# One more step of lookahead in the down stage of a feed-forward, with squares written later and the powers of the norm begun sooner

## The chip, the core and the metric

The kernel runs on one core of a Trainium2 chip. The core has TensorE (PE: matmuls and transposes, 128 x 128 weights against up to 512 columns), VectorE (DVE), ScalarE (ACT), GpSimd (POOL) and SyncE (SP, which issues loads and stores). Each engine works through a queue of its own in order, and a semaphore holds an instruction until what it needs is there. The metric is the device time of one execution in microseconds, the median of several runs.

## The reference

512 tokens of width 1024 pass through two layers. A layer is a feed-forward, a group of four token mixers, and a second feed-forward, each behind an RMS norm and added to x:

```python
def rmsnorm(x, g):
    xf = x.astype(jnp.float32)
    y = xf * lax.rsqrt(jnp.mean(xf * xf, axis=-1, keepdims=True) + EPS)
    return (y * g.astype(jnp.float32)).astype(x.dtype)

def swiglu(h, w1, w3, w2):
    return (jax.nn.silu(h @ w1) * (h @ w3)) @ w2

for l in range(DEPTH):                       # DEPTH = 2
    h = rmsnorm(x, ffn1_norm[l])
    x = x + FFN_RESIDUAL * swiglu(h, ffn1_w1[l], ffn1_w3[l], ffn1_w2[l])   # 0.5; w2 is 2816 x 1024
    h = rmsnorm(x, mix_norm[l])
    ...                                      # four token mixers, added to x
    h = rmsnorm(x, ffn2_norm[l])
    x = x + FFN_RESIDUAL * swiglu(h, ffn2_w1[l], ffn2_w3[l], ffn2_w2[l])
return rmsnorm(x, final_norm)
```

## The kernel before

**Stages.** The four feed-forwards are called f0a, f0b, f1a and f1b (layer, first or second). Each has an up stage (w1 and w3 with the gate) and a down stage (w2). After f0a and f1a come the mixers of the layer (L0, L1), after f1b the last norm and the store. x is held as four blocks of 128 tokens, x0 to x3.

**Precision.** Every float32 product is made of three: an operand is split into a rounded part, hi, by a cast on ScalarE, and the rest, lo, by a subtraction on VectorE, and TensorE adds hi·hi, hi·lo and lo·hi (lines 107 to 109). So each piece of weights costs a cast whi, a split wlo, and for the activations a cast and a split `as`, all before its matmuls can start.

**The down stage.** The product with w2 is cut into halves of tokens and of output columns and made with seven products in place of eight, called a to g, whose operands are quarters of w2 or sums of them. A quarter has 11 rows of 128, taken in six pieces j (`SUB`: five of two rows, one of one). So there are 42 steps (product, piece), in the order a0 a1 b0 a2 b1 ... b5, d and e in the same way, c and f in the same way, then g0 to g5. A full step is 12 matmuls of 512 columns, one with the last piece 6.

Before a step's matmuls three things happen to its weights. `fetch` has SyncE load a raw quarter piece into one of six places (tag `raw`, shared with the up stage). `presum` adds on VectorE what is a sum: for b the raw pieces of a and b into a tile tt, for c the raw pieces c and h, for f the activations. `prepare` makes the splits, whi and wlo into three places each. For b and d it also has GpSimd issue an accumulating load onto tt, which makes the weights of a later product. In the loop over steps s the calls are `fetch(s + 6)`, `presum(s + 4)`, `prepare(s + 2)`, `product(s)`, `joins(s)`.

`joins(s)` adds finished products from PSUM (tiles px, pz, pw, pr) to x, half the columns of a block at a time (`add`), has ScalarE square what of x is final and sum it by rows (`square`), and begins the next norm: `scale` adds the two sums of squares (nv, VectorE), raises that to −1/2 (ry, GpSimd, `rsqrt`) and scales the block (xn, VectorE). Behind g3 the blocks 2 and 3 are transposed on TensorE (`turn`, pt; in f1b there is no norm to feed, and no transpose). Then g4 and g5 are done for one block of tokens after the other, each followed by its add, square and `scale` (in f1b by `last`, which scales and stores).

**What sets the order.** Within a down stage the order on VectorE and ScalarE is that of the calls (`manual_schedule`), and so it is on TensorE in the whole program. `s_` and `sn` in the tables are operands of the gate of the up stage, `raw_f0a9..` and `wlo_f0a9..` weights of its last step.

Of the kernel before, what the change touches and what calls it, by code (L numbers as in the profile page):

```python
# [15 lines left out]
P = 128  # L16
# [33 lines left out]
def trunk(ctx: ExitStack, tc: tile.TileContext, x, par, gains, tab, w13, w2, wi, wg, wo, out):  # L50
# [61 lines left out]
    def rsqrt(v, n, name):  # L112
        y = small.tile([P, n], F32, tag=f"ry{n}", name=f"ry_{name}")
        G.tensor_tensor(y, v, expo[:, 0:n], ALU.pow)
        return y


    class Norm:
# [3 lines left out]
        def __init__(self, name, index):  # L122
            self.name, self.index = name, index
            self.quarters = index % 3 != 1
            self.ss, self.xn = {}, {}
            self.gain = None
            self.op = {}
            self.t = {}
# [11 lines left out]

        def scale(self, b):
            with tc.high_priority(offset=400):
                if self.gain is None:
                    self.gain = first_gain if self.index == 0 else load_gain(self.index)
                v = small.tile([P, 1], F32, tag="nv", name=f"nv_{self.name}{b}", bufs=4)
                ss = self.ss[b]
                V.tensor_scalar(v, ss[:, 0:1], ss[:, 1:2], EPS, ALU.add, ALU.add)
                y = rsqrt(v, 1, f"{self.name}{b}")
                xn = tmp.tile([P, D], F32, tag="xn", name=f"xn_{self.name}{b}")
                V.scalar_tensor_tensor(xn, xt[b], y, self.gain, ALU.mult, ALU.mult)  # L150
                self.xn[b] = xn
# [219 lines left out]
    def down(f, a, s1, s2, nxt, name, end=False):  # L371
# [53 lines left out]
        def prepare(s):  # L425
# [16 lines left out]
            raw = tview(j) if m in "bdf" else raws[m, j]  # L442
            whi = wts.tile([P, n, T], F32R, tag="whi", name=f"whi_{name}{m}{j}")
            wlo = wts.tile([P, n, T], F32R, tag="wlo", name=f"wlo_{name}{m}{j}")
            S.copy(whi, raw)
# [31 lines left out]
        def joins(s):  # L477
# [5 lines left out]
            elif (m, j) == ("d", 0):  # L483
                for t in range(2):
                    add(1, 1, t, "z", 1)
            elif (m, j) == ("d", last):
                for t in range(2):
                    add(0, 1, t, "x", -1)
            elif (m, j) == ("c", 1):
                for t in range(2):  # L490
                    add(0, 0, t, "w", 1)
                    nxt.square(t, 0)
            elif (m, j) == ("c", last):
                for t in range(2):
                    add(1, 1, t, "x", -1)
                    nxt.square(2 + t, 1)
                    add(1, 0, t, "x", 1)
            elif (m, j) == ("f", last):
                for t in range(2):
                    add(1, 0, t, "r", 1)  # L500
                    nxt.square(2 + t, 0)
            elif m == "g" and j < 2:
                if end:
                    nxt.last(2 + j)
                else:
                    nxt.scale(2 + j)

        with tc.manual_schedule(engines={mybir.EngineType.DVE, mybir.EngineType.Activation}):
            for s in range(6):
                fetch(s)  # L510
            for s in range(2):
                prepare(s)
            for s in range(2, 4):
                presum(s)
            tail = len(steps) - 2
            for s in range(tail):
                fetch(s + 6)
                presum(s + 4)
                prepare(s + 2)
                product(s)  # L520
# [4 lines left out]
            for t in range(2):  # L525
                for s in (tail, tail + 1):
                    product(s, (t,))
                add(0, 1, t, "z", 1)
                nxt.square(t, 1)
                if end:  # L530
                    nxt.last(t)
# [427 lines left out]
```

## Time and profile before

| what | value |
|---|---|
| median of three runs | 1709.82 us |
| the three runs | 1709.77, 1709.82, 2012.91 us |
| profiled execution, its own time | 1710.36 us |
| its span in the trace | 1708.7 us |
| busy, share of the span: PE, PEld, DVE, ACT, POOL | 97%, 89%, 77%, 50%, 8% |
| chain that ended last, by engine | PE 83%, DVE 10%, issue 3%, ACT 3%, DMA 1% |
| mean DMA rate | 166 GB/s |

The profile shows one execution. Busy shares are taken over the whole span. A matmul's record overlaps the next one, so its start is the surer time. In the chain of waits each piece is followed back to what released it; "issue" is time in which an engine waited for nothing that the profile shows. The run of 2012.91 us stands alone.

### The profile page before, as it was taken

Reading aid. Unit: us, or ns where it says so; the run is one execution under the profiler, and the core shown is the slowest. Engines: PE = TensorE matmul, PEld = TensorE weight load, DVE = VectorE, ACT = ScalarE, POOL = GpSimd, SP = SyncE. Lnnn points to the kernel's source line nnn. Section 1 sums busy time; section 2 is a strip of 40 time slices with the busy share of each in tenths; the row PEclk is TensorE's granted clock in tenths of the full one; section 3 lists DMA queues with packets and bytes.
Section 4 is the critical chain, followed back from the end, with each engine's and each line's share of the span. In section 5 each row is a group of like instructions: output and inputs, shape, how many; then the busy total and the mean of one; then the engine's idle time right before and its main releaser. Section 6 shows DMA issues by size and latency. Waiting matters only on the chain.

```text
span 1708.7 us, 27504 instructions
## 1 busy us (share of the span) xinstructions
PE 1661.4 (97%) x11072; PEld 1517.7 (89%) x11072; DVE 1310.9 (77%) x1661; ACT 850.0 (50%) x1238; POOL 140.2 (8%) x170
## 2 busy tenths in 40 slices
PE   8999999989999999999999999999999999999997
PEld 8999998778779999988699999886887799999875
DVE  5777778879856777788887777888796577777986
ACT  5454555553344554556554554555433455545554
POOL 1000002010010001001000000010000101000100
PEclk9999999999999999999999999999999999999999
DMA  6776669543332777769457777694323346776872
GB/s 199 190 181 173 174 173 263 179 154 100 111 86 71 183 194 185 183 191 258 131 137 182 191 183 190 186 258 160 124 89 97 87 122 183 181 186 181 228 220 82
DMA packets 80479, 283.94 MB, mean 166 GB/s; under 512 B 8928, under 2 KB 9056, under 8 KB 80352
## 3 DMA queue, kind: packets, MB, share of 16 engines
q1 hardware_dynamic: 61920, 217.18, 38.7%
q0 software_dynamic: 18432, 65.02, 21.9%
q8 instruction: 86, 1.41, 0.3%
q14 instruction: 41, 0.34, 0.1%
HBM read 280.07 MB, written 2.10 MB: 165 GB/s over the span
## 4 chain that ended last, share of the span: by engine, by line
PE 83%; DVE 10%; issue 3%; ACT 3%; DMA 1%; POOL 0%; POOLq 0%; ACTq 0%; DVEq 0%; SPq 0%
PE pi_L L108 3%; PE pi_L L107 3%; PE pi_L L109 3%; PE px_f1b L109 3%; PE px_f1a L109 3%; PE px_f0a L109 3%; PE px_f1b L107 3%; PE px_f1a L107 3%; PE px_f0a L107 3%; PE px_f0a L108 3%; PE px_f1b L108 3%; PE px_f1a L108 3%; PE px_f0b L109 3%; PE px_f0b L107 3%; PE px_f0b L108 3%
## 5 line engine op out<-in xcount | busy, mean ns | idle before, releaser
L107 PE MATMUL pi_L<-gh_m,whi_L1i 128*128 128x512 f32 (+1 forms) x128 | 47.5, 371 | 0.3 <-ACT gh_m L183 0.3
L107 PE MATMUL pi_L<-gh_m,whi_L0i 128*128 128x512 f32 (+1 forms) x128 | 47.5, 371 | 0.3 <-ACT gh_m L183 0.3
L108 PE MATMUL pi_L<-gl_m,whi_L0i 128*128 128x512 f32 (+1 forms) x128 | 46.6, 364 | 0.6 <-DVE gl_m L184 0.6
L108 PE MATMUL pi_L<-gl_m,whi_L1i 128*128 128x512 f32 (+1 forms) x128 | 46.6, 364 | 0.6 <-DVE gl_m L184 0.6
L109 PE MATMUL pi_L<-gh_m,wlo_L1i 128*128 128x512 f32 (+1 forms) x128 | 46.4, 363 | 0.0
L109 PE MATMUL pi_L<-gh_m,wlo_L0i 128*128 128x512 f32 (+1 forms) x128 | 46.4, 363 | 0.0
L770 DVE SCALAR_TENSOR_TENSOR scr_gv_L<-scr_cv_L,pt,scr_gv_L 128x511 f32<-128x511 f32 (+29 forms) x60 | 43.8, 731 | 0.6
L770 DVE SCALAR_TENSOR_TENSOR scr_cv_L<-scr_cv_L,pt,scr_cv_L 128x511 f32<-128x511 f32 (+29 forms) x60 | 43.7, 728 | 0.1
L107 PEld LDWEIGHTS pi_L<-gh_m,whi_L0i 128*128 128x128 f32 x128 | 24.2, 189 | 4.9 <-ACT gh_m L183 0.6
L108 PEld LDWEIGHTS pi_L<-gl_m,whi_L1i 128*128 128x128 f32 x128 | 24.2, 189 | 4.8 <-DVE gl_m L184 0.8
L108 PEld LDWEIGHTS pi_L<-gl_m,whi_L0i 128*128 128x128 f32 x128 | 24.2, 189 | 4.8 <-DVE gl_m L184 0.8
L107 PEld LDWEIGHTS pi_L<-gh_m,whi_L1i 128*128 128x128 f32 x128 | 24.2, 189 | 4.8 <-ACT gh_m L183 0.6
L97 ACT CAST whi_L1i<-raw_L1i 128x1024 fp32r<-128x1024 f32 x14 | 14.6, 1050 | 27.3 <-PE pi_L L108 16.4
L97 ACT CAST whi_L0i<-raw_L0i 128x1024 fp32r<-128x1024 f32 x14 | 14.6, 1049 | 27.3 <-PE pi_L L108 16.4
L109 PEld LDWEIGHTS pi_L<-gh_m,wlo_L1i 128*128 128x128 f32 x128 | 24.2, 189 | 3.8
L109 PEld LDWEIGHTS pi_L<-gh_m,wlo_L0i 128*128 128x128 f32 x128 | 24.2, 189 | 3.8
L136 ACT ACTIVATE sq_a<-x 128x512 f32<-128x512 f32 x16 | 10.1, 632 | 29.3 <-DVE x L475 29.2
L205 DVE TENSOR_TENSOR B_b<-pt_b,B_b 128x512 fp32r<-128x512 f32 x16 | 10.1, 681 | 18.5 <-ACT B_b L204 18.5
L108 PE MATMUL p_f0b<-B_b,whi_f0b 128*128 128x256 f32 x64 | 19.4, 303 | 2.9 <-DVE B_b L205 2.9
L136 ACT ACTIVATE sq_m<-x 128x512 f32<-128x512 f32 x16 | 10.1, 632 | 24.0 <-DVE x L475 23.9
L108 PE MATMUL p_f1b<-B_b,whi_f1b 128*128 128x256 f32 x64 | 19.0, 298 | 2.8 <-DVE B_b L205 2.8
L107 PE MATMUL p_f0b<-B_b,whi_f0b 128*128 128x256 f32 x64 | 19.2, 300 | 2.5 <-ACT B_b L204 2.5
(3183 smaller groups left out, 7303.2 us busy)
## 6 DMA issues: line engine op xcount, KB each, us to landing
raw_L0i<-wi SPq DMA_DIRECT2D x14, 512.0 KB, 3.7
raw_L1i<-wi SPq DMA_DIRECT2D x14, 512.0 KB, 3.7
tt_f0a<-w POOLq DMA_DIRECT2D x10, 512.0 KB, 7.2
tt_f0b<-w POOLq DMA_DIRECT2D x10, 512.0 KB, 7.8
tt_f1a<-w POOLq DMA_DIRECT2D x10, 512.0 KB, 7.6
tt_f1b<-w POOLq DMA_DIRECT2D x10, 512.0 KB, 8.4
gain<-gains SPq DMA_DIRECT2D x7, 512.0 KB, 4.1
raw_L0o<-wo SPq DMA_DIRECT2D x6, 512.0 KB, 3.9
```

What stands on the lines that cost most here:

```text
L97: S.copy(hi, raw)
L107: PE.matmul(ps, sh, mh, start=first, stop=False, skip_group_check=more)
L108: PE.matmul(ps, sh, ml, start=False, stop=False, skip_group_check=more)
L109: PE.matmul(ps, sl, mh, start=False, stop=last, skip_group_check=more)
L136: S.activation(sq, xt[b][:, c * T : (c + 1) * T], AF.Square, scale=1.0 / 32.0, accum_out=self.ss[b][:, c : c + 1],)
L205: V.tensor_tensor(lo[:, :, s], ps[q], hi[:, :, s].bitcast(F32), ALU.subtract)
L770: V.scalar_tensor_tensor(acc[:, kk:], v[:, : T - kk], cw, acc[:, kk:], ALU.mult, ALU.add)
```

## The change

- The split weights of every fourth step (s % 4 == 3) go to a fourth place, the tile `q3` of another pool, which holds an operand of the up stage before. `prepare` works three steps ahead, `fetch` seven and `presum` five; the raw places stay six.
- At the start three steps are prepared instead of two, and the first sums (of b) stand ahead of them.
- The add of w moves from c1 to c2, its squares to c3. After c's last step both pairs of adds come together, and their squares follow f's last but one step. After f's last step both adds come first, then the squares.
- `scale` is cut in two, `root` (sum and power) and the scaling. For blocks 2 and 3 both roots are called at g0 and both scalings at g1. At the end of the stage the root of block 0 is called ahead of block 1's last matmuls, and both scalings (or `last`) come behind those.
- The powers have four places.

```diff
--- before.py
+++ after.py
@@ -110,7 +110,7 @@
 
 
     def rsqrt(v, n, name):
-        y = small.tile([P, n], F32, tag=f"ry{n}", name=f"ry_{name}")
+        y = small.tile([P, n], F32, tag=f"ry{n}", name=f"ry_{name}", bufs=4)
         G.tensor_tensor(y, v, expo[:, 0:n], ALU.pow)
         return y
 
@@ -122,7 +122,7 @@
         def __init__(self, name, index):
             self.name, self.index = name, index
             self.quarters = index % 3 != 1
-            self.ss, self.xn = {}, {}
+            self.ss, self.y, self.xn = {}, {}, {}
             self.gain = None
             self.op = {}
             self.t = {}
@@ -138,16 +138,22 @@
                     accum_out=self.ss[b][:, c : c + 1],
                 )
 
-        def scale(self, b):
+        def root(self, b):
+
             with tc.high_priority(offset=400):
                 if self.gain is None:
                     self.gain = first_gain if self.index == 0 else load_gain(self.index)
                 v = small.tile([P, 1], F32, tag="nv", name=f"nv_{self.name}{b}", bufs=4)
                 ss = self.ss[b]
                 V.tensor_scalar(v, ss[:, 0:1], ss[:, 1:2], EPS, ALU.add, ALU.add)
-                y = rsqrt(v, 1, f"{self.name}{b}")
+                self.y[b] = rsqrt(v, 1, f"{self.name}{b}")
+
+        def scale(self, b):
+            if b not in self.y:
+                self.root(b)
+            with tc.high_priority(offset=400):
                 xn = tmp.tile([P, D], F32, tag="xn", name=f"xn_{self.name}{b}")
-                V.scalar_tensor_tensor(xn, xt[b], y, self.gain, ALU.mult, ALU.mult)
+                V.scalar_tensor_tensor(xn, xt[b], self.y[b], self.gain, ALU.mult, ALU.mult)
                 self.xn[b] = xn
 
         def turned(self, b, q):
@@ -440,8 +446,13 @@
             t = asplits[-1]
             hi, lo = (t[:, s % 2, x, : n * 256].rearrange("p (n t) -> p n t", n=n) for x in range(2))
             raw = tview(j) if m in "bdf" else raws[m, j]
-            whi = wts.tile([P, n, T], F32R, tag="whi", name=f"whi_{name}{m}{j}")
-            wlo = wts.tile([P, n, T], F32R, tag="wlo", name=f"wlo_{name}{m}{j}")
+            if s % 4 == 3:
+
+                w = acts.tile([P, 2, n, T], F32R, tag="q3", name=f"w_{name}{m}{j}")
+                whi, wlo = w[:, 0], w[:, 1]
+            else:
+                whi = wts.tile([P, n, T], F32R, tag="whi", name=f"whi_{name}{m}{j}")
+                wlo = wts.tile([P, n, T], F32R, tag="wlo", name=f"wlo_{name}{m}{j}")
             S.copy(whi, raw)
             S.copy(hi, src)
             V.tensor_tensor(wlo, raw, whi.bitcast(F32), ALU.subtract)
@@ -486,37 +497,47 @@
             elif (m, j) == ("d", last):
                 for t in range(2):
                     add(0, 1, t, "x", -1)
-            elif (m, j) == ("c", 1):
+            elif (m, j) == ("c", 2):
                 for t in range(2):
                     add(0, 0, t, "w", 1)
+            elif (m, j) == ("c", 3):
+                for t in range(2):
                     nxt.square(t, 0)
             elif (m, j) == ("c", last):
                 for t in range(2):
                     add(1, 1, t, "x", -1)
+                for t in range(2):
+                    add(1, 0, t, "x", 1)
+            elif (m, j) == ("f", last - 1):
+                for t in range(2):
                     nxt.square(2 + t, 1)
-                    add(1, 0, t, "x", 1)
             elif (m, j) == ("f", last):
                 for t in range(2):
                     add(1, 0, t, "r", 1)
+                for t in range(2):
                     nxt.square(2 + t, 0)
-            elif m == "g" and j < 2:
-                if end:
-                    nxt.last(2 + j)
-                else:
-                    nxt.scale(2 + j)
+            elif (m, j) == ("g", 0):
+                for t in range(2):
+                    nxt.root(2 + t)
+            elif (m, j) == ("g", 1):
+                for t in range(2):
+                    if end:
+                        nxt.last(2 + t)
+                    else:
+                        nxt.scale(2 + t)
 
         with tc.manual_schedule(engines={mybir.EngineType.DVE, mybir.EngineType.Activation}):
-            for s in range(6):
+            for s in range(7):
                 fetch(s)
-            for s in range(2):
+            for s in range(2, 5):
+                presum(s)
+            for s in range(3):
                 prepare(s)
-            for s in range(2, 4):
-                presum(s)
             tail = len(steps) - 2
             for s in range(tail):
-                fetch(s + 6)
-                presum(s + 4)
-                prepare(s + 2)
+                fetch(s + 7)
+                presum(s + 5)
+                prepare(s + 3)
                 product(s)
                 joins(s)
             if not end:
@@ -527,6 +548,9 @@
                     product(s, (t,))
                 add(0, 1, t, "z", 1)
                 nxt.square(t, 1)
+                if t == 0:
+                    nxt.root(t)
+            for t in range(2):
                 if end:
                     nxt.last(t)
                 else:
```

The matmuls are the same in the same order. VectorE's queue at the entry of f0a's down stage: `wlo_f0a9..`, `s5_f0a9` belong to the last step of the up stage, `tt0` is the first sum for b, `raw_f0aa1`, `raw_f0ab1` loads of pieces of a and b. Before:

```order
L349 TENSOR_TENSOR sn_f0a9_2615<-pw_f0a9_2613,sn_f0a9_2615 128x512
L99 TENSOR_TENSOR wlo_f0a9e_2739<-raw_f0a9e_2607,whi_f0a9e_2737 128x1024
L312 TENSOR_TENSOR a04_f0a_225<-sn_f0a9_2615 128x256
L99 TENSOR_TENSOR wlo_f0a9f_2770<-raw_f0a9b_2605,whi_f0a9f_2768 128x1024
L99 TENSOR_TENSOR wlo_f0a9g_2801<-raw_f0a9g_2610,whi_f0a9g_2799 128x1024
L356 TENSOR_TENSOR s5_f0a9_2616<-px_f0a9_2612,s5_f0a9_2616 128x512
L447 TENSOR_TENSOR wlo_f0aa0_2853<-raw_f0aa0_2839,whi_f0aa0_2852 128x1024
```

After, where the sums `tt0` (b0 and b1) stand ahead of f's split of the last up step and of `s5`:

```order
L318 TENSOR_TENSOR a04_f0a_225<-sn_f0a9_2615 128x256
L425 TENSOR_TENSOR tt0_f0a_2834<-raw_f0aa0_2839,raw_f0ab0_2843 128x1024
L99 TENSOR_TENSOR wlo_f0a9f_2770<-raw_f0a9b_2605,whi_f0a9f_2768 128x1024
L99 TENSOR_TENSOR wlo_f0a9g_2801<-raw_f0a9g_2610,whi_f0a9g_2799 128x1024
L425 TENSOR_TENSOR tt0_f0a_2834<-raw_f0aa1_2841,raw_f0ab1_2847 128x1024
L362 TENSOR_TENSOR s5_f0a9_2616<-px_f0a9_2612,s5_f0a9_2616 128x512
L458 TENSOR_TENSOR wlo_f0aa0_2857<-raw_f0aa0_2839,whi_f0aa0_2856 128x1024
```

Before, both sums came behind the first splits of a; what now stands behind them is the rest of the last up step.

ScalarE's queue in f0a from f's last cast on: `sq_m0xy` is the square of block x, columns y, for the mixers' norm, `whi_L0g0` the mixers' first weights. Before:

```order
L445 CAST whi_f0af5_3559<-tt2_f0a_2836 128x512
L446 CAST as_f0af4_3538<-a15_f0a_232 128x256
L136 ACTIVATE sq_m021_3573,ss_m02_3572<-x2_83 128x512
L136 ACTIVATE sq_m031_3578,ss_m03_3577<-x3_84 128x512
L445 CAST whi_f0ag0_3584<-raw_f0ag0_3493 128x1024
L446 CAST as_f0ag0_3583<-s_f0a0_974 128x512
L445 CAST whi_f0ag1_3604<-raw_f0ag1_3515 128x1024
L446 CAST as_f0ag0_3583<-s_f0a1_1438 128x512
L136 ACTIVATE sq_m020_3617,ss_m02_3572<-x2_83 128x512
L97 CAST whi_L0g0_3787<-raw_L0g0_3785 128x1024
L136 ACTIVATE sq_m030_3620,ss_m03_3577<-x3_84 128x512
L445 CAST whi_f0ag2_3623<-raw_f0ag2_3536 128x1024
```

After:

```order
L456 CAST w_f0af5_3539<-tt2_f0a_2836 128x512
L457 CAST as_f0af4_3518<-a15_f0a_232 128x256
L456 CAST whi_f0ag0_3559<-raw_f0ag0_3467 128x1024
L457 CAST as_f0ag0_3558<-s_f0a0_974 128x512
L456 CAST whi_f0ag1_3577<-raw_f0ag1_3495 128x1024
L457 CAST as_f0ag0_3558<-s_f0a1_1438 128x512
L136 ACTIVATE sq_m021_3596,ss_m02_3595<-x2_83 128x512
L136 ACTIVATE sq_m031_3599,ss_m03_3598<-x3_84 128x512
L456 CAST whi_f0ag2_3602<-raw_f0ag2_3516 128x1024
L457 CAST as_f0ag2_3601<-s_f0a2_1902 128x512
L97 CAST whi_L0g0_3777<-raw_L0g0_3775 128x1024
L136 ACTIVATE sq_m020_3616,ss_m02_3595<-x2_83 128x512
```

The squares of the columns 1 stood ahead of the cast for g0 and stand now behind that for g1; the cast for the mixers stands behind that for g2.

VectorE's queue in f0a about the norm of blocks 2 and 3 (`nv`, `xn`). Before:

```order
L447 TENSOR_TENSOR wlo_f0ag2_3624<-raw_f0ag2_3536,whi_f0ag2_3623 128x1024
L448 TENSOR_TENSOR as_f0ag2_3622<-s_f0a2_1902,as_f0ag2_3622 128x512
L147 TENSOR_SCALAR nv_m02_3643<-ss_m02_3572 128x1
L150 SCALAR_TENSOR_TENSOR xn_m02_3647<-x2_83,ry_m02_3645,gain1_3641 128x1024
L447 TENSOR_TENSOR wlo_f0ag3_3650<-raw_f0ag3_3557,whi_f0ag3_3649 128x1024
L448 TENSOR_TENSOR as_f0ag2_3622<-s_f0a3_2366,as_f0ag2_3622 128x512
L147 TENSOR_SCALAR nv_m03_3667<-ss_m03_3577 128x1
L150 SCALAR_TENSOR_TENSOR xn_m03_3671<-x3_84,ry_m03_3669,gain1_3641 128x1024
L447 TENSOR_TENSOR wlo_f0ag4_3675<-raw_f0ag4_3581,whi_f0ag4_3674 128x1024
```

After:

```order
L458 TENSOR_TENSOR w_f0ag3_3620<-raw_f0ag3_3537,w_f0ag3_3620 128x1024
L459 TENSOR_TENSOR as_f0ag2_3601<-s_f0a3_2366,as_f0ag2_3601 128x512
L148 TENSOR_SCALAR nv_m02_3639<-ss_m02_3595 128x1
L148 TENSOR_SCALAR nv_m03_3643<-ss_m03_3598 128x1
L458 TENSOR_TENSOR wlo_f0ag4_3649<-raw_f0ag4_3556,whi_f0ag4_3648 128x1024
L459 TENSOR_TENSOR as_f0ag4_3647<-s_f0a4_2830,as_f0ag4_3647 128x512
L156 SCALAR_TENSOR_TENSOR xn_m02_3666<-x2_83,ry_m02_3641,gain1_3637 128x1024
L156 SCALAR_TENSOR_TENSOR xn_m03_3668<-x3_84,ry_m03_3645,gain1_3637 128x1024
```

Both sums now come ahead of g4's split, and both scalings behind it, one after the other.

## Rows read from the trace of the kernel before

**Rows 1.** Windows, f0a by pairs of products: us, busy (instructions) by engine, granted clock, DMA:

```profile
248.18:279.17 30.99, 30.65 (x135) 24.71 (x134) 28.01 (x36) 17.36 (x25) 6.11 (x7) 1.00 0.88 256
279.17:309.08 29.91, 29.91 (x133) 24.77 (x132) 24.58 (x31) 17.43 (x25) 4.37 (x5) 1.00 0.98 240
309.08:343.82 34.74, 32.85 (x137) 24.94 (x135) 30.91 (x41) 20.28 (x33) 0.00 (x0) 1.00 0.45 141
343.82:364.03 20.21, 17.52 (x80) 13.36 (x79) 16.75 (x23) 11.17 (x19) 2.83 (x3) 1.00 0.70 221
```

**Rows 2.** Windows of the down stages f0b, f1a and f1b:

```profile
745.52:859.92 114.40, 111.11 (x481) 87.79 (x479) 98.69 (x126) 67.27 (x102) 11.50 (x14) 1.00 0.69 194
1089.10:1205.27 116.17, 111.99 (x480) 89.00 (x479) 100.67 (x128) 66.66 (x102) 13.12 (x15) 0.99 0.73 211
1585.87:1699.48 113.61, 109.83 (x464) 85.81 (x462) 95.99 (x123) 62.57 (x95) 11.50 (x15) 1.00 0.66 185
```

**Rows 3.** Chain of waits in f0a: start, us, what:

```profile
358.35 1.75 PE pt_m L157 x16
```

**Rows 4.** Timeline of TensorE in f0a, around f0 and g0:

```profile
320.19 0.39 PE L109 MATMUL px_f0a<-whi_f0ac,as_f0af 128*128 128x512 f32 x1
...
323.04 0.39 PE L107 MATMUL pr_f0a<-whi_f0af,as_f0af 128*128 128x512 f32 x1
...
341.34 0.39 PE L109 MATMUL pr_f0a<-whi_f0af,as_f0af 128*128 128x512 f32 x1
...
343.82 0.40 PE L107 MATMUL pz_f0a<-whi_f0ag,as_f0ag 128*128 128x512 f32 x1
```

**Rows 5.** Timeline of ScalarE in f0a, from f to g (in brackets: idle before, releaser):

```profile
318.36 0.63 ACT L136 ACTIVATE sq_m<-x 128x512 f32<-128x512 f32 x1 [4.45 <-DVE x L475]
...
319.75 1.03 ACT L445 CAST whi_f0af<-tt_f0a 128x1024 fp32r<-128x1024 f32 x1
...
340.53 1.03 ACT L445 CAST whi_f0ag<-raw_f0ag 128x1024 fp32r<-128x1024 f32 x1
...
346.93 1.05 ACT L97 CAST whi_L0g<-raw_L0g 128x1024 fp32r<-128x1024 f32 x1 [0.35 <-DMA raw_L0g<-wg]
```

**Rows 6.** Timeline of VectorE in f0a, before f:

```profile
315.91 1.21 DVE L447 TENSOR_TENSOR wlo_f0ac<-raw_f0ac,whi_f0ac 128x1024 fp32r<-128x1024 f32 x1
317.05 0.68 DVE L448 TENSOR_TENSOR as_f0af<-a_f0a,as_f0af 128x512 fp32r<-128x512 f32 x1
317.65 1.28 DVE L475 SCALAR_TENSOR_TENSOR x<-pw_f0a,x 128x512 f32<-128x512 f32 x2
```

**Rows 7.** Timeline of VectorE at the end of f1b:

```profile
1697.62 0.69 DVE L475 SCALAR_TENSOR_TENSOR x<-pz_f1b,x 128x512 f32<-128x512 f32 x1 [1.06 <-PE pz_f1b L109]
...
1700.05 1.28 DVE L150 SCALAR_TENSOR_TENSOR xn_a<-x,ry_a,gain 128x1024 f32<-128x1024 f32 x1 [0.73 <-POOL ry_a L114]
...
1703.72 1.28 DVE L150 SCALAR_TENSOR_TENSOR xn_a<-x,ry_a,gain 128x1024 f32<-128x1024 f32 x1 [0.73 <-POOL ry_a L114]
```

**Rows 8.** Timeline of GpSimd, powers of the norm after f0a:

```profile
364.94 0.55 POOL L114 TENSOR_TENSOR ry_m<-nv_m,expo 128x1 f32<-128x1 f32 x1 [8.39 <-DVE nv_m L147]
368.81 1.39 POOL L114 TENSOR_TENSOR ry_m<-nv_m,expo 128x1 f32<-128x1 f32 x1 [3.32 <-DVE nv_m L147]
```

**Rows 9.** Timeline of SyncE's queue, VectorE and TensorE at f0a's entry:

```profile
233.36 0.33 SPq L91 DMA_DIRECT2D raw_f0ab<-w  x1
...
237.88 1.23 DVE L99 TENSOR_TENSOR wlo_f0a9f<-raw_f0a9b,whi_f0a9f 128x1024 fp32r<-128x1024 f32 x1 [1.37 <-ACT whi_f0a9f L97]
...
245.30 0.28 PE L107 MATMUL px_f0a<-T_n,whi_f0a9g 128*128 128x256 f32 x1
```

**Rows 10.** DMA issues from 233 to 234: KB, us to landing:

```profile
raw_f0ab<-w SPq DMA_DIRECT2D x1, 512.0 KB, 4.5
```

**Rows 11.** Tile raw_f0aa, six loads:

```profile
DMA to landing us min/median/max: 3.4/4.1/8.4
```

**Rows 12.** Window in g of f1a:

```profile
1192.93:1196.33 3.40, 3.40 (x9) 2.63 (x9) 2.81 (x3) 0.88 (x2) 0.56 (x1) 0.50 0.65 190
```

## Prediction

> **What bounds the kernel now.** I read the windows of the four down stages first, because all edits but the one at the very end lie in them. In each, TensorE is busy for 110 to 112 of 114 to 116 us, and no other engine passes 101 (for f0a the sum of its four rows) [rows 1, 2]: the matmuls are the bound, and the question is only what they lose. Busy time hides that, since a matmul's record (0.39 us) is longer than the distance to the next, so I go by starts. For f0a the windows are cut by pairs of products: a/b, d/e, c/f and g. The pair d/e runs 132 matmuls in 29.91 us without a wait, which is a pace of 0.2266. A stage has 462, so 104.69 us, and three of the four have 16 transposes as well, 1.75 [rows 3]. Against that:
>
> f0a 115.85 − 104.69 − 1.75 = 9.41; f0b 114.40 − 106.44 = 7.96; f1a 116.17 − 106.44 = 9.73; f1b, without transposes, 113.61 − 104.69 = 8.92 [rows 1, 2]. Together **36.0 us** are lost, and that is the most that the stages can give back.
>
> By pairs in f0a: a/b loses 30.99 − 29.91 = 1.08; c/f, whose window reaches three matmuls into g, 34.74 − 29.91 − 0.68 = 4.15; g the remaining 4.18. The timeline of TensorE shows two of these waits in full: from the last matmul of c's first steps to the fourth of f's first step 2.85 us pass where four paces (0.91) would do, a loss of **1.94**; from f's end to the fourth matmul of g's first step 2.48, a loss of **1.57** [rows 4].
>
> ScalarE's timeline says why. The cast of f's weights, which TensorE is waiting for, starts at 319.75, behind two squares (the first at 318.36), for which ScalarE had waited 4.45 us on an add of VectorE. The cast of g's first weights starts at 340.53, again behind squares. In g, the cast of the weights of the following mixer (346.93) waited for its load, with g's third cast queued behind it [rows 5]. So these are not engines short of time but queues in which something late stands ahead of something wanted, with only two products (24 matmuls, 5.44 us) of work prepared ahead to cover it.
>
> **The change part by part.** It adds and removes no matmul, cast, split or transfer. An add or a square is 0.6 to 0.7 us whether early or late [rows 5, 6], and nothing here costs time of its own.
>
> *Fourth place, preparing three steps ahead.* Cover goes from 24 to 36 matmuls, 8.16 us, so 2.72 more before a late split is felt. The place is the tile of the up stage's operand T4, so its first cast waits for the last up product, over at 248.18 [rows 1], and is due 36 matmuls later: no cost. Each wait above is under 3: f 1.94, g0 1.57, and in g 4.18 for two waits together. On its own that takes off most of each.
>
> *Squares and adds moved.* The add of w goes one step of c on and its squares another one; by then f's first casts are past, which removes what stood at 318.36 [rows 5]. The squares after c's last step go behind f's last but one, so they no longer stand ahead of g's first cast. Their cost stays hidden behind ScalarE's idle time: it is busy for 20.28 of 34.74 in c/f [rows 1]. If that cover were gone, one square would delay one cast by 0.7.
>
> *Norm begun sooner.* The sums and powers of blocks 2 and 3 are issued at g's first step and used one step later. On VectorE 0.2 for a sum moves ahead of g's fifth split, and the power has that split (1.14 + 0.60 from the starts in [rows 6]) to run beside. What remains is VectorE's own work between the end of c and the transposes: four adds (0.60 each, two of them take 1.28 [rows 6]), g's splits 1 to 4 at 1.74, two adds of r, the mixer's split 1.14, two sums 0.3 (one with its hand-overs is under 2.43 − 0.60 − 0.70 − 0.73 = 0.40, by the round in [rows 7]) and the scaling of block 2, 1.28 [rows 7]: 2.4 + 6.96 + 1.2 + 1.14 + 0.3 + 1.28 = 13.3. TensorE in the meantime has f's last two steps and four of g, 2.72 + 1.36 + 10.88 = 14.96. A margin of 1.7 is thin, for VectorE catches up hardly at all in c/f: a pair of steps costs it 2 × 1.74 + 1.14 + 0.60 = 5.22 per 5.44 of TensorE, and the adds of w (1.2) come on top. I allow a wait of **1.0 at each of the three turns**, between 0 (margin kept) and 3.0 (VectorE comes to the four adds behind by those of w and two splits, 1.2 + 3.48 = 4.7, and the margin takes 1.7 of it). This is what is late next. On SyncE one load of the mixer's weights moves ahead of a table's, on GpSimd in f1a one power (0.55) ahead of the issue of an accumulating load; in the stage nothing waits for what is put behind them.
>
> Speaking against it is one more row: a power alone on GpSimd takes 0.55, beside a split on VectorE it took 1.39 [rows 8], and both now run beside a split. The first needs 1.39 of 1.74, the second 2.78 of the 2.94 until its scaling, so at this price both stay hidden, and the sum holds nothing for it. The Trainium skill ("SBUF — State Buffer", section "Who interferes with whom") says that a VectorE instruction with two SBUF inputs contends with a GpSimd instruction that reads SBUF, and that whoever comes first can block the other wholly. The row agrees that it slows; it was not blocked until the split's end and 0.55 more. If it were, each turn would come some 0.8 later and the total would be some 2.4 higher.
>
> *First sums of b placed ahead of the first splits.* This adds waits. The sum of b0 now stands in VectorE's queue ahead of the split of the up stage's product f, that of b1 ahead of s5, the last but one gate's operand. In f0a the load that b0 needs is issued at 233.36 and lands 4.5 later [rows 9, 10], at 237.9, when that split would start (237.88): split and everything behind it move by 1.17. The load for b1 needs the place that this split frees, so it is issued at about 240.25; with a landing time L, sum and s5 are done at 240.25 + L + 1.14 + 0.60 + 0.1, and TensorE's last up product into X, which overwrites what s5 reads, wants to start at 245.30 [rows 9]. The wait is L − 3.2: at L = 4.1, the middle for this ring [rows 11], 0.9; at 3.4, 0.2. For it the 1.08 of a/b goes, which was a wait for the split of b0. I take **0.8** left in f0a and in f1a, whose entries look alike, and 0.1 in f0b and f1b, where the trace has the first of these loads landed before the split is due: 1.8 in all.
>
> *End.* The sum of block 1's last piece no longer stands behind the scaling of block 0. Before: add 1697.62, scaling of block 0 at 1700.05 (2.43 for add, square, sum and power), scaling of block 1 at 1703.72 [rows 7]. After, the last add can start when the matmuls end, 1699.5 to 1699.7, and 2.43 later, at 1702.1 to 1702.2, its scaling, by when that of block 0 is over. **1.5** less; 0 if the store binds.
>
> *Sum.* 36.0 lost; 1.8 stays at the entries, 3.0 at the turns, and 0.4 a stage (1.6) that I count as no wait, most of what c/f keeps in f0a when f and g0 are taken off (4.15 − 1.94 − 1.57 = 0.64). Gain 36.0 − 6.4 + 1.5 = 31.1. The profiled execution took 1710.36, so 1679.3; it was 0.54 above the median, so **1679** against 1709.82.
>
> **The rivals.** *Half of it.* Only the order of the queues helps: f and g0 go, (1.94 + 1.57) × 4 = 14.0, plus 1.5 at the end, so 1694. For it: the loads still share six places, and a step fetched sooner waits for its place; and in g a cast stood behind a load [rows 5], which more places don't bring sooner. Against: loads of this ring land in 4.1 at the middle [rows 11], less than the 8.16 ahead.
>
> *Slower: the entry.* The wait L − 3.2 in all four stages. It decides at the point where it eats a stage's gain of 7.4: L = 10.6. At 12 it costs 8.8 × 4 = 35, so 1679 + 35 = 1714. For it: a load of this ring took 8.4 [rows 11]. Against: the two in question land in less than half of 10.6.
>
> *It doesn't do what it says.* The third step ahead is prepared no sooner, since its weights aren't there or VectorE is late by as much, and the moved adds make waits of their own: the end's 1.5 and the wait of f in two of the stages (3.9) go, so 1704.
>
> *The clock.* In g of f1a TensorE was granted 0.50, its level of 1.2 GHz, for 3.40 us right behind a wait [rows 12], which is 1.7 lost; f0a's like wait passed without it. The sum has this 1.7 among f1a's 9.73. It comes back if the clock falls elsewhere: plus or minus 1.7, no case by itself.
>
> **How the numbers follow.** The forecast, 1674 to 1687, 0.74: at the lower end no turn waits and no entry does (−4.8), at the upper one turns keep 3.0 (6.0 more) and the two entries wait for an L of 4.5 (1.3 each, 1.0 more). The half, 1688 to 1699, 0.15. Not what it says, 1700 to 1711, 0.07. Slower through the entry, over 1711, 0.04. The range, 1674 to 1697, holds nearly all of the first and most of the second. A difference of 2%, 34 us, is about what a measurement of this kernel can tell from no change: faster than that is under 1675.6, and even all 36.0 with the end would give 1672, so 0.07; slower by over 2% needs an L above 19, 0.02; within, 0.91.
>
> **What would show it.** Right: stages of 107 to 109 us, c/f without a wait above 0.5, squares on ScalarE with casts of f and g ahead of them, at the turns a wait of under 1.5 with VectorE as the releaser, scaling of block 1 within 2.7 of the last matmul. Wrong: a cast of f or g that starts after TensorE came to wait for it; a product of the last up step waiting on s5 by more than 1; a power of over 1.5.

## Result

The changed kernel takes 1681.21 us, median of four runs (1680.16 to 1681.79), against 1710.67 of the kernel before (four runs, one of them the lone 2012.91, which is left out of the ratio). The ratio is **0.9824, interval 0.981 to 0.9837**: 29.5 us less. The forecast was 1679, the range 1674 to 1697. The profiled execution took 1681.03, its span is 1679.3. The prediction takes 2% for about what a measurement can tell; the four runs here lie within 1.7 us of each other, so 29.5 is told apart easily.

The windows of the four down stages, from the first matmul to the last (columns as in [rows 1]):

```profile
248.37:356.68 108.31, 107.07 (x481) 88.25 (x479) 98.39 (x129) 66.86 (x102) 13.79 (x15) 1.00 0.76 215
738.35:846.67 108.32, 107.09 (x480) 88.28 (x479) 96.99 (x127) 67.34 (x102) 13.06 (x14) 1.00 0.71 194
1075.17:1183.48 108.31, 107.07 (x481) 88.25 (x479) 98.46 (x129) 66.77 (x102) 13.67 (x15) 1.00 0.77 216
1564.82:1671.44 106.62, 105.25 (x464) 86.38 (x462) 93.72 (x123) 62.37 (x95) 13.06 (x14) 1.00 0.68 186
```

Against [rows 1, 2] they are shorter by 7.54 (the rows of f0a summed), 6.08, 7.86 and 6.99, **28.5** in all. By the same sum as in the prediction (104.69 of pace, 1.75 of transposes) they now lose 1.87, 1.88, 1.87 and 1.93, 7.55 together, where they lost 36.0. The granted clock is 1.00 in all four, so the stretch of [rows 12] is gone. By pairs of products in f0a:

```profile
248.37:278.32 29.95, 29.95 (x135) 24.78 (x133) 27.43 (x37) 18.70 (x27) 6.12 (x7) 1.00 0.86 227
278.32:308.24 29.92, 29.92 (x134) 24.77 (x132) 25.04 (x33) 17.33 (x25) 4.38 (x5) 1.00 1.01 268
308.24:338.16 29.92, 29.92 (x134) 24.77 (x132) 28.53 (x40) 19.15 (x32) 0.00 (x0) 1.00 0.49 147
338.16:356.68 18.52, 17.28 (x84) 13.91 (x82) 17.39 (x25) 11.68 (x21) 3.29 (x3) 1.00 0.66 220
```

a/b and c/f now run at the pace of d/e to within 0.05 us: the waits at b0, at f and at g0 are gone entirely. What is left lies in g. There the timeline of TensorE shows one wait, at the transposes; in f1b, which has none, one at g's last split:

```profile
350.44 2.29 PE L163 MATMUL pt_m<-ident,xn_m 128*128 128x128 f32 x16 [1.13 <-DVE xn_m L156]
```

```profile
1668.69 0.50 PE L108 MATMUL pz_f1b<-wlo_f1bg,as_f1bg 128*128 128x512 f32 x1 [1.37 <-DVE wlo_f1bg L458]
```

By starts the first is 1.30, and 0.31 more before the second block's transposes, 1.61 at each of three turns; the other is 1.53. Together 6.4 of the 7.55.

At the end, the same rows of VectorE as [rows 7]:

```profile
1669.56 0.69 DVE L486 SCALAR_TENSOR_TENSOR x<-pz_f1b,x 128x512 f32<-128x512 f32 x1 [0.59 <-PE pz_f1b L109]
...
1671.65 0.69 DVE L486 SCALAR_TENSOR_TENSOR x<-pz_f1b,x 128x512 f32<-128x512 f32 x1 [0.33 <-PE pz_f1b L109]
1672.26 1.27 DVE L156 SCALAR_TENSOR_TENSOR xn_a<-x,ry_a,gain 128x1024 f32<-128x1024 f32 x1
1673.45 0.21 DVE L148 TENSOR_SCALAR nv_a<-ss_a 128x1 f32<-128x1 f32 x1
1674.38 1.28 DVE L156 SCALAR_TENSOR_TENSOR xn_a<-x,ry_a,gain 128x1024 f32<-128x1024 f32 x1 [0.73 <-POOL ry_a L114]
```

From the end of the matmuls to the last scaling it is now 2.94 (1674.38 − 1671.44), it was 4.24 (1703.72 − 1699.48), and from there to the end of the span 7.86 against 9.2: 1.35 less. The ledger of the spans: 28.5 from the stages and 1.35 from the end, less 0.4 by which the rest of the program is longer, make the 29.4 between 1708.7 and 1679.3. The clock explains that 0.4 and more: at the entry of f1b's up stage, behind a wait, TensorE's matmuls ran at half clock for 3.40 us before and run so for 4.70 now, 0.65 more of loss. The window before, then after:

```profile
1356.77:1360.17 3.40, 3.40 (x17) 3.40 (x17) 2.18 (x3) 2.09 (x4) 0.00 (x0) 0.50 0.43 154
```

```profile
1335.13:1339.83 4.70, 4.70 (x24) 4.70 (x23) 2.94 (x4) 2.41 (x4) 0.00 (x0) 0.50 0.30 108
```

### The profile page after: what moved, and what is told of

Its sections match the earlier page's. It is cut to its first block, busy times and chain, and to the rows that moved or that the text cites. A ratio compares the mean times of both kernels' runs of the same rounds, so it can differ in the third digit from the quotient of the medians.

```text
span 1679.3 us, 27504 instructions
## 1 busy us (share of the span) xinstructions
PE 1645.1 (98%) x11072; PEld 1520.0 (91%) x11072; DVE 1307.3 (78%) x1661; ACT 850.0 (51%) x1238; POOL 145.5 (9%) x170
## 3 DMA queue, kind: packets, MB, share of 16 engines
q8 instruction: 86, 1.41, 0.3%
## 4 chain that ended last, share of the span: by engine, by line
PE 91%; DVE 5%; issue 1%; ACT 1%; POOL 1%; DMA 0%; POOLq 0%; DVEq 0%; ACTq 0%
PE px_f0b L107 3%; PE px_f1b L107 3%; PE px_f1a L107 3%; PE px_f1a L108 3%; PE px_f0a L108 3%; PE px_f0a L109 3%; PE px_f0b L109 3%; PE px_f1b L109 3%; PE px_f0a L107 3%; PE px_f1b L108 3%; PE px_f0b L108 3%; PE px_f1a L109 3%; PE pi_L L108 3%; PE pi_L L107 3%; PE pi_L L109 3%; PE pz_f1a L107 2%
## 5 line engine op out<-in xcount | busy, mean ns | idle before, releaser
L108 PE MATMUL p_f1b<-B_b,whi_f1b 128*128 128x256 f32 x64 | 19.4, 304 | 2.8 <-DVE B_b L211 2.8
L107 PE MATMUL p_f1b<-B_b,whi_f1b 128*128 128x256 f32 x64 | 19.3, 302 | 2.2 <-ACT B_b L210 2.2
L107 PE MATMUL p_f0a<-B_n,whi_f0a 128*128 128x256 f32 x64 | 18.9, 295 | 2.1 <-ACT whi_f0a L278 1.8
```

Of the source, the lines that this page charges most:

```text
L107: PE.matmul(ps, sh, mh, start=first, stop=False, skip_group_check=more)
L108: PE.matmul(ps, sh, ml, start=False, stop=False, skip_group_check=more)
```

## Experiments

Two questions stayed open. The change does three things at once: it adds cover (one more step prepared ahead), puts the queues within a stage in another order, and does the same at the entry. Which of them takes which wait? And why does each turn wait 1.61 where the sum had 1.0, and f1b 1.53 where it had nothing? Each kernel is a small edit; times are medians of four runs, of the last experiment a single one. The kernel before, measured beside them, took 1711.38 (lookahead alone, order alone, and the two on sum and power and on the scalings) and 1711.17 (the others), where it took 1710.67 beside the changed kernel; so a difference of times from the changed kernel is sure to some 0.7 us.

**Lookahead alone.** The changed kernel with the old `joins`, the old end of the stage and the old first lines of the loop:

```diff
             for s in range(7):
                 fetch(s)
-            for s in range(2, 5):
-                presum(s)
-            for s in range(3):
-                prepare(s)
+            for s in range(2):
+                prepare(s)
+            for s in range(2, 5):
+                presum(s)
+            prepare(2)
...
-            elif (m, j) == ("c", 2):
+            elif (m, j) == ("c", 1):
                 for t in range(2):
                     add(0, 0, t, "w", 1)
-            elif (m, j) == ("c", 3):
-                for t in range(2):
                     nxt.square(t, 0)
...
```

> The fourth place and one more step of lookahead alone; adds, squares, norm, the end of the stage and the first sums of b as before. If cover is what counts (36 matmuls prepared ahead outlast any wait under 2.7), the waits at f and at g0 go, g keeps about 4.2 - 2.7 = 1.5, the entry keeps its 1.0, and the end nothing: some 6 us in each of four stages, so about 1686. If the order of the queues is what counts, casts still stand behind the squares, f and g0 keep half, and it comes to 1697 or more.

Measured: 1702.31, ratio 0.995 (0.9935 to 0.9965), 9 us. Neither theory fits: the time is where order had it (1697 or more), but not for its reason. As cover had it, the waits at f and g0 are gone, but for 0.2 to 0.5 a stage. But g keeps more than 1.5: in f0a its fourth product waits 1.59 by starts, and then the turn waits 2.74 for the second scaling. TensorE's timeline in f0a:

```profile
349.15 0.49 PE L107 MATMUL pz_f0a<-w_f0ag,as_f0ag 128*128 128x512 f32 x1 [0.54 <-ACT as_f0ag L457]
349.89 0.49 PE L108 MATMUL pz_f0a<-w_f0ag,as_f0ag 128*128 128x512 f32 x1 [0.24 <-DVE w_f0ag L458]
...
352.92 1.04 PE L163 MATMUL pt_m<-ident,xn_m 128*128 128x128 f32 x8
356.53 1.09 PE L163 MATMUL pt_m<-ident,xn_m 128*128 128x128 f32 x8 [2.58 <-DVE xn_m L156]
```

In VectorE's queue block 3's scaling stands behind g's fifth split, and each power holds the queue for 0.73 while nothing else there can run, as in [rows 7]:

```profile
351.31 1.28 DVE L156 SCALAR_TENSOR_TENSOR xn_m<-x,ry_m,gain 128x1024 f32<-128x1024 f32 x1 [0.74 <-POOL ry_m L114]
352.51 1.22 DVE L458 TENSOR_TENSOR wlo_f0ag<-raw_f0ag,whi_f0ag 128x1024 fp32r<-128x1024 f32 x1
...
355.19 1.29 DVE L156 SCALAR_TENSOR_TENSOR xn_m<-x,ry_m,gain 128x1024 f32<-128x1024 f32 x1 [0.73 <-POOL ry_m L114]
```

More places for split weights don't help against that. Here the clock fell behind the wait, too, 3.41 us at 0.50 in f0a.

**Order alone.** The new `joins`, `root` and end, with three places, two steps of lookahead and the old entry:

```diff
-            if s % 4 == 3:
-
-                w = acts.tile([P, 2, n, T], F32R, tag="q3", name=f"w_{name}{m}{j}")
-                whi, wlo = w[:, 0], w[:, 1]
-            else:
-                whi = wts.tile(...)
-                wlo = wts.tile(...)
+            whi = wts.tile(...)
+            wlo = wts.tile(...)
...
-                fetch(s + 7)
-                presum(s + 5)
-                prepare(s + 3)
+                fetch(s + 6)
+                presum(s + 4)
+                prepare(s + 2)
```

> The moved adds and squares, the norm begun sooner and the end alone; three places and two steps of lookahead, first sums as before. If cover is what counts, only f (1.94) and g0 (1.57) go in each stage, 14 in all, and 1.4 at the end: about 1695. If order counts, the waits in g shrink as well, since the sums of the norm no longer stand ahead of g's splits: 1685 or less.

Measured: 1693.91, ratio 0.9898 (0.9883 to 0.9913), 17.5 us, near what cover expected. The waits at f and g0 are gone here too, but for 0.4 a stage. g's third product still waits, by starts 2.9 us in f0a, 2.7 in f1a and 1.1 in each of the other two:

```profile
348.50 0.50 PE L107 MATMUL pz_f0a<-whi_f0ag,as_f0ag 128*128 128x512 f32 x1 [1.42 <-ACT as_f0ag L452]
```

For f0a and f1a, where the mixers follow, ScalarE's timeline has the reason, another one of the same kind: the last squares of r, which wait 2.47 for their adds, and the mixer's cast stand ahead of g's third cast.

```profile
344.19 0.63 ACT L136 ACTIVATE sq_m<-x 128x512 f32<-128x512 f32 x1 [2.47 <-DVE x L481]
...
345.32 1.05 ACT L97 CAST whi_L0g<-raw_L0g 128x1024 fp32r<-128x1024 f32 x1 [0.41 <-DMA raw_L0g<-wg]
346.28 0.62 ACT L136 ACTIVATE sq_m<-x 128x512 f32<-128x512 f32 x1
...
346.90 1.03 ACT L451 CAST whi_f0ag<-raw_f0ag 128x1024 fp32r<-128x1024 f32 x1
```

So the two parts do not share the waits out between them. Each alone takes nearly all of those at f and g0, 14.0 by the prediction's sum, and each leaves waits of its own in g. The windows of the four stages, 460.0 together before, are 449.6 with the lookahead alone, 444.2 with the order alone and 431.6 with the change. The forecast's own rival, that order alone would do half (1694), is near what order alone does.

**The entry put back.** The changed kernel with the first sums of b behind two splits:

```diff
-            for s in range(2, 5):
-                presum(s)
-            for s in range(3):
-                prepare(s)
+            for s in range(2):
+                prepare(s)
+            for s in range(2, 5):
+                presum(s)
+            prepare(2)
```

> The changed kernel with the first sums of b behind the first two splits of a again, as before the change. If placing them ahead is what took b's first wait, it comes back at each of the four entries (about 0.9 of waiting, 1.1 with what follows): about 4.3 us more, 1685.5. If the added step of lookahead took it, nothing changes, 1681, and the order of the entry was worth nothing.

Measured: 1685.73, ratio 0.9851 (0.9837 to 0.9866), 4.5 more than the changed kernel. Each stage is longer by 1.03 to 1.06, and b0's split is again what TensorE waits for:

```profile
255.57 0.50 PE L108 MATMUL pz_f0a<-wlo_f0ab,as_f0ab 128*128 128x512 f32 x1 [0.24 <-DVE wlo_f0ab L458]
```

The wait of a/b was thus taken by the order of the entry and not by cover. With 9.1 and 17.5 the three parts come to 31.1 one by one, and to 29.5 to 30 together. That is no sign that they are independent: the waits at f and g0 are counted in both of the first two, and most of that is made up by waits in g that go only when both are there.

**The end put back.** The changed kernel with `last` or `scale` of each block directly behind its add, as before:

```diff
                 nxt.square(t, 1)
-                if t == 0:
-                    nxt.root(t)
-            for t in range(2):
                 if end:
                     nxt.last(t)
                 else:
                     nxt.scale(t)
```

> The changed kernel with the end of the stage as before: block 0's scaling ahead of block 1's last add. If the 1.35 us between the last matmul and the end came from this order alone, they come back: 1682.6. If they came from elsewhere (the store, the clock), 1681.

Measured: 1682.48, ratio 0.9833 (0.9817 to 0.9849). The time alone can't tell 1.3 us; the trace does, with 1681.4 − 1672.12 = 9.28 from the end of the matmuls to the end of the span against 7.86, while the stages lose what they lose in the changed kernel (7.56 against 7.55).

**Sum and power one step sooner.** The changed kernel with `root` of blocks 2 and 3 directly behind the last squares:

```diff
             elif (m, j) == ("f", last):
                 for t in range(2):
                     add(1, 0, t, "r", 1)
                 for t in range(2):
                     nxt.square(2 + t, 0)
-            elif (m, j) == ("g", 0):
                 for t in range(2):
                     nxt.root(2 + t)
```

> The changed kernel with sum and power of blocks 2 and 3 one step sooner, behind the last squares, so that the first power runs before a split of weights does. If the power of 2.13 us was held by the split beside it, it takes about 0.55 now, the scaling starts 0.46 sooner, and the wait at each turn goes from 1.61 to 1.15: about 1.8 us less over four stages, 1679.4. If VectorE is merely behind with its own work and the power filled a gap that is there anyway, nothing changes: 1681.

Measured: 1677.67, ratio 0.9804 (0.9788 to 0.9821), 3.5 less than the changed kernel, twice the 1.8. In the changed kernel the power of block 2 runs beside a split of weights and one of activations and ends only 0.4 behind the second; then comes the scaling, whose queue has waited 0.46 for it. Its timeline of GpSimd, and of VectorE beside it:

```profile
346.94 2.13 POOL L114 TENSOR_TENSOR ry_m<-nv_m,expo 128x1 f32<-128x1 f32 x1 [3.85 <-DVE nv_m L148]
```

```profile
344.84 1.23 DVE L458 TENSOR_TENSOR w_f0ag<-raw_f0ag,w_f0ag 128x1024 fp32r<-128x1024 f32 x1 [0.67 <-ACT w_f0ag L456]
345.98 0.68 DVE L459 TENSOR_TENSOR as_f0ag<-s_f0a,as_f0ag 128x512 fp32r<-128x512 f32 x1
346.59 0.33 DVE L148 TENSOR_SCALAR nv_m<-ss_m 128x1 f32<-128x1 f32 x2
346.83 1.21 DVE L458 TENSOR_TENSOR wlo_f0ag<-raw_f0ag,whi_f0ag 128x1024 fp32r<-128x1024 f32 x1
347.96 0.68 DVE L459 TENSOR_TENSOR as_f0ag<-s_f0a,as_f0ag 128x512 fp32r<-128x512 f32 x1
349.11 2.48 DVE L156 SCALAR_TENSOR_TENSOR xn_m<-x,ry_m,gain 128x1024 f32<-128x1024 f32 x2 [0.46 <-POOL ry_m L114]
```

In the run of the experiment the first power begins before the next split and takes 0.56, and the scaling starts without a wait. Its VectorE, and TensorE at the turn:

```profile
344.70 0.32 DVE L148 TENSOR_SCALAR nv_m<-ss_m 128x1 f32<-128x1 f32 x2
345.35 1.22 DVE L458 TENSOR_TENSOR w_f0ag<-raw_f0ag,w_f0ag 128x1024 fp32r<-128x1024 f32 x1 [0.33 <-ACT w_f0ag L456]
```

```profile
350.17 2.07 PE L163 MATMUL pt_m<-ident,xn_m 128*128 128x128 f32 x14 [0.37 <-DVE xn_m L156]
```

TensorE waits 0.37 at the turn in f0a where it waited 1.13, and each stage is 0.75 to 0.80 shorter, 3.1 of the 3.5: 0.46 of it is the power, and the other 0.3 the two sums themselves, which now run in the gap of 0.67 (0.33 of it is left) instead of ahead of a split. The expectation had left the sums out.

**Scalings ahead of g's fifth split.** As the run before, and:

```diff
-            elif (m, j) == ("g", 1):
+            elif (m, j) == (("g", 2) if end else ("g", 0)):
                 for t in range(2):
                     if end:
                         nxt.last(2 + t)
                     else:
                         nxt.scale(2 + t)
```

> As the run before, and the scalings of blocks 2 and 3 ahead of g's fifth split; in the last stage, which has no transposes, behind g's last split. If the turns wait for VectorE because two scalings come behind a split that is not yet needed, all four late waits go (3 x 1.61 + 1.53 = 6.4): about 1675. If VectorE is simply short of time there, the wait moves behind the transposes, to g's fifth split, and the time stays at 1680 to 1681.

Measured: **1674.61**, ratio 0.9787 (0.9772 to 0.9802), 6.6 less than the changed kernel and the fastest of all. TensorE is busy in every part of the four stages:

```profile
249.05:355.70 106.65, 106.65 (x480) 88.35 (x479) 97.45 (x128) 66.19 (x100) 12.21 (x15) 1.00 0.78 218
737.31:843.92 106.61, 106.61 (x480) 88.38 (x479) 95.92 (x124) 67.20 (x102) 11.49 (x14) 1.00 0.71 195
1073.65:1180.28 106.63, 106.63 (x480) 88.32 (x479) 97.77 (x128) 66.17 (x101) 12.07 (x15) 1.00 0.77 219
1560.81:1665.62 104.81, 104.81 (x464) 86.48 (x462) 93.50 (x122) 62.35 (x95) 11.48 (x14) 1.00 0.68 186
```

They lose 0.7 together, against 36.0 and 7.55. Of the 6.6, 3.1 come on top of the run before (1677.67); the scalings alone, with sums and powers where the change has them, were not tried. VectorE was thus not short of time at the turns; a split that wasn't due yet stood ahead of the scalings that were.

**New order everywhere, two steps of lookahead.** As the kernel with the order alone, but with the sums of b ahead of the first splits, squares of r and roots at g0, scalings at g1 (in f1b at g3):

```diff
             elif (m, j) == ("f", last):
                 for t in range(2):
                     add(1, 0, t, "r", 1)
+            elif (m, j) == ("g", 0):
                 for t in range(2):
                     nxt.square(2 + t, 0)
-            elif (m, j) == ("g", 0):
                 for t in range(2):
                     nxt.root(2 + t)
-            elif (m, j) == ("g", 1):
+            elif (m, j) == (("g", 3) if end else ("g", 1)):
```

> Three places and two steps of lookahead with the new order everywhere: first sums ahead, squares of r behind the third cast of g, sum and power behind them, scaling behind g's fourth split (in the last stage behind all). If the order is what counts and the fourth place only covers what is left, a stage loses 1 to 2, some 1678. If two steps can't cover VectorE's work between the end of c and the turns, each stage keeps 3 to 4: about 1687.

Measured: 1679.40, ratio 0.9814 (0.9799 to 0.9829). The stages lose 1.83, 1.22, 1.62 and 1.20. Without the fourth place, and with each queue in the order in which its work is due, the kernel is at the level of the changed one. The fourth place then gives some 5 us more (1674.61), if each of the two orders is about the best for its number of places, which wasn't tried.

**Thirty more powers.** The changed kernel with powers that nobody needs:

```diff
                 for t in range(2):
                     add(0, 1, t, "x", -1)
+                probe = small.tile([P, 1], F32, tag="probe", name=f"probe_{name}", bufs=1)
+                for _ in range(30):
+                    G.tensor_tensor(probe, xt[0][:, T : T + 1], expo[:, 0:1], ALU.pow)
```

> The changed kernel with 30 more powers of one column on GpSimd in each down stage, back to back from the last add of d on, with nothing waiting for them. If a power is held by a VectorE instruction that reads two operands from SBUF, one that begins in a split lasts until the split ends and 0.4 to 0.55 more, up to 1.8, and one beside an add that reads PSUM takes 0.55. If GpSimd is only slowed by whatever VectorE does, all powers beside work take about the same, 1.2 to 1.5. VectorE's splits stay at 1.21 if GpSimd is always the one that yields.

One run: 1681.39. The tile's view in f0a:

```profile
L502 POOL TENSOR_TENSOR probe_f0a<-x,expo x30: 549/556/1412, 306.9 to 332.6; 128x1 f32<-128x1 f32 x30
```

The median is the 0.55 of a power alone, the longest 1.41. The long ones (13 of 30 over 1.0, and one of 0.85) ended some 0.4 behind the end of a split or sum of two operands from SBUF, in which all but one of them had begun; the short ones began in the last 0.12 us of such an instruction, or in an add that reads PSUM. GpSimd's work slowed VectorE by little: the splits wlo_f0af took 1233 ns in the mean instead of 1214, and the stages lose 7.50, as before. So a power is held by the one instruction that was running, and by no fixed factor. In the same execution the power of the norm took 2.18, held by two splits in a row, which none of the 30 was. With the order alone, it was held by the first of the same two splits in f0a and f1a (1.53) and by both in f0b and f1b (2.13). What decides whether it gets in between stays open.

## Why the prediction was right

The time was 2.2 above the forecast, 29.5 us gained where 31.1 had been forecast; the other 0.6 is that the median of the kernel before came out 0.85 higher, less what the forecast had rounded up. The mechanism was the one given: waits of TensorE on casts that stood behind late squares and adds. That the sum came so near is in part luck, for two of its errors cancel: 1.8 too much at the entries, 1.8 too little at the turns. By its terms:

- *36.0 to be had in the stages.* 28.5 were gained, 29.6 forecast. The term for what is left was 6.4 and measured 7.55.
- *The fourth place on its own.* The prediction had it take off most of each wait. That holds for f and g0, not for g: alone it took 10.4 of the 36.0.
- *Entry, 1.8 left.* Mis-sized: nothing is left, a/b runs at the pace. The rule L − 3.2 took the second load to be issued when the up stage's split ends (240.25). It was issued at 239.45, when the sum of b0, which stands ahead of that split, ended and freed a place, and landed 3.55 later. VectorE's timeline at the entry:

```profile
238.20 1.23 DVE L425 TENSOR_TENSOR tt_f0a<-raw_f0aa,raw_f0ab 128x1024 f32<-128x1024 f32 x1 [1.51 <-DMA raw_f0ab<-w]
239.34 1.22 DVE L99 TENSOR_TENSOR wlo_f0a9f<-raw_f0a9b,whi_f0a9f 128x1024 fp32r<-128x1024 f32 x1
...
243.03 1.22 DVE L425 TENSOR_TENSOR tt_f0a<-raw_f0aa,raw_f0ab 128x1024 f32<-128x1024 f32 x1 [0.87 <-DMA raw_f0ab<-w]
244.17 0.68 DVE L362 TENSOR_TENSOR s_f0a<-px_f0a,s_f0a 128x512 f32<-128x512 f32 x1
```

  VectorE did wait for both loads, 1.51 and 0.87, but the operand of the gate was read by 244.85, and TensorE's product came at 245.49. The rival that ends slower starts from the same point, so its L is about 11.6 instead of 10.6 (the load was issued 0.80 sooner, and the product came 0.19 later); the loads took 4.56 and 3.55.
- *Turns, 3.0.* Mis-sized: 4.8, the main error with the next point. The sum's margin of 1.7 was used up exactly by VectorE starting the four adds 1.67 behind the end of c (335.75 against 334.08). TensorE's first matmul behind c, then ScalarE and VectorE:

```profile
334.08 0.39 PE L107 MATMUL pr_f0a<-whi_f0af,as_f0af 128*128 128x512 f32 x1
```

```profile
332.92 1.05 ACT L456 CAST whi_f0ag<-raw_f0ag 128x1024 fp32r<-128x1024 f32 x1 [1.79 <-PE pr_f0a L109]
```

```profile
334.00 1.23 DVE L458 TENSOR_TENSOR wlo_f0ag<-raw_f0ag,whi_f0ag 128x1024 fp32r<-128x1024 f32 x1 [1.39 <-ACT whi_f0ag L456]
...
335.75 2.48 DVE L486 SCALAR_TENSOR_TENSOR x<-px_f0a,x 128x512 f32<-128x512 f32 x4
```

  It was not late with its own work, as the prediction had feared: it had waited 1.39 for g's first cast, which had waited 1.79 for a place, and the adds stood behind the two splits of that step, whose matmuls begin only at 338.16. On top came two waits that the sum didn't have, 0.67 for g's fourth cast, which stands behind the squares of r, and 0.46 for the power; and 0.31 is the second scaling, which the sum left out.
- *The power.* This step failed in its reading of a row. I took 1.39 in [rows 8] for a slowing, since it was less than the time to the split's end and 0.55 more. But the power was blocked until that end, and only what follows is shorter, 0.4: the split ended at 369.79, the power at 370.20. VectorE's row there, in the kernel before:

```profile
368.58 1.21 DVE L99 TENSOR_TENSOR wlo_L0i<-raw_L0i,whi_L0i 128x1024 fp32r<-128x1024 f32 x1
```

  So the sum held nothing for it, and in the changed kernel the power took 2.13, held by two splits; a power of over 1.5 was one of the prediction's signs of being wrong. It cost 0.46 in each stage. The Trainium skill ("SBUF — State Buffer", section "Who interferes with whom") says that a VectorE instruction with two SBUF inputs contends with a GpSimd instruction that reads SBUF, and the trace agrees: 1.40 and 2.13 beside splits, 0.55 alone or beside an add from PSUM. The prediction's price for it was 2.4 in all; the wait for the power was 4 × 0.46 = 1.8.
- *f1b.* The sum had no turn there and so no wait. But the same two scalings stand there, ahead of g's last split, which TensorE reaches sooner without transposes: 1.53.
- *No wait, 1.6.* 7.55 − 4.83 − 1.53 = 1.2.
- *End, 1.5.* 1.35. The last scaling began 2.94 behind the last matmul and not within 2.7: block 1's sum (1673.45) stood behind block 0's scaling in VectorE's queue, some 0.3 later than its square allowed.
- *The clock.* The 1.7 in f1a went as the sum had it; 0.65 came back at f1b's entry.

The rival "half of it" lost because its ground, shared raw places, didn't matter: with the third step prepared, TensorE waits for no cast in a, b, c, d, e or f. As a statement on the order of the queues alone it came near, 17.5 us gained where it had 15.5; 1693.91 meets its 1694 in part because the kernel before took 1711.38 beside it.

## To carry to other kernels

Where several engines feed a matmul, look in each queue for the instruction that waits, and for what is queued behind it that is due sooner; putting each queue in the order in which its results are due gave nearly all here (1679.4 with no more memory), and a deeper lookahead the last 5, if both orders are about the best. A deeper lookahead also puts splits that aren't due yet ahead of work that is: the changed kernel was left waiting at just such places, and moving two sums with their powers one step ahead and two scalings ahead of one split gave another 6.6.

## What was not expected of the hardware

A one-column power on GpSimd, 0.55 alone, if it begins well before the end of a VectorE instruction with two SBUF operands, lasts until that end and 0.4 more: 1.40 behind one split, 2.13 behind two in a row, the latter in all four stages of the changed kernel. VectorE hardly notices such powers (1233 against 1214 ns a split with GpSimd at it all the time). A longer instruction of GpSimd it does notice: the split of the mixer's first weights, 1.21 to 1.23 where no such instruction runs, took 1.35 in f0a of the changed kernel, where it began in a select of 0.64, and 1.62 in the run with thirty powers; both ended 1.1 behind the select.
